# Warm-up products and weight rooms in the opening, spare memory for weights and gated-attention loads, rounded masks and values two blocks behind in a one-core decoder step

## The chip, the cores and the metric

The kernel runs on one core of one Trainium2 chip. The metric is device time in microseconds (us) of one execution, as the median of several. A core has a matrix engine (TensorE, in the profile PE for its products and PEld for its weight loads), a vector engine (VectorE, DVE), a scalar engine (ScalarE, ACT), GpSimd (POOL), and SyncE (SP), which here only issues DMAs. Each engine works through its own instructions in the order in which the program holds them.

## The reference

One step of a decoder layer, for a prompt of 1024 rows and for 8 sequences of 8 new rows over a paged cache of 8192 positions (64 blocks of 128 positions for each sequence):

```
n = rmsnorm(h, g_mix);  u = n @ w_in          # one projection; columns: gq gk gv gg ga mq mkv mkr
z = ga @ gla_w_a2 + gla_b_a                   # gate of the gated linear attention
o_gla = gla_chunked(gq, gk, gv, log_sigmoid(z) / 16, state)
cq = rmsnorm(mq);  q = rope(rmsnorm(cq @ mla_w_qup));  ckv = rmsnorm(mkv);  krope = rope(rmsnorm(mkr))
k, v = latent_to_kv(ckv, krope, mla_w_kvup)
o_mla = prompt_attention(q, k, v)             # causal, prompt;  sample_attention over the paged cache for the 64 sample rows
h = h + concat(o_gla, o_mla) @ w_o
h = h + conv_ffn(rmsnorm(h));  h = h + (p @ ple_w_proj) * sigmoid(rmsnorm(h) @ ple_w_gate)
```

`ga`, `mq`, `mkv` and `mkr` together are 432 columns of `w_in`, called the latents below (`NL` = 432).

## The kernel before

Everything is float32. A product of full precision is made of three products of rounded halves: an operand x is split into a high part (`act.copy` into the type fp32r, F32R in the code) and a low part (x minus the high part, on DVE or POOL), and high x high, high x low and low x high are added up in PSUM (`mm3`, L139 to L141).

Two streams of work are interleaved. `cache_stream()` walks the 64 cache blocks of the sample attention (tiles `craw`, `ctp`, `cTh`/`cTl`, `ks`, `csr`, `mt`, `cpv`). `dense()` does all other work as generators that yield between steps: the opening and the first half of the prompt (`prompt_half(0)`), the second half (`prompt_half(1)`), gated linear attention (`gla_sample`, `gla_prompt`), `prompt_attention`, the output projection, then, from about 1340 us on, the feed-forward layer and the tail. A table `PACE` says how much dense work goes beside a cache block. The program written so is then put in order, for each engine, by the Tile scheduler at build time, which places instructions by its own estimates of when operands are ready; so an edit in one place can move instructions far from it.

The parts that the change touches:

- **The opening.** `sample_x` (L336) loads and normalises the 64 sample rows and transposes them (`pt`, `transpose_split` L128) into `xTs`. `load_lat` (L259) loads the 432 latent columns of `w_in` in eight pieces of 128 rows through a `stage` buffer, of which there are three: a piece is loaded (L266), its high part copied by ACT (L267), its low part made by DVE or POOL in turn (L271), and only then is the buffer free for a piece three further on. `sample_u` (L344) multiplies the sample rows with these weights (`ps_sm`), `proj_lat` (L741) each prompt tile (`ps_lt`), k by k with all three products. Both come out of `mm_lat` (L274, matmul L278). The sample rows then go through a chain of their own: latents, `ps_qs` (L390), norms and rotation on DVE and ACT (`q_finish`), transposes `pt_q` (L416), products `ps_qp` (L420).
- **The mix chunks.** `proj` multiplies 512 prompt columns with a chunk of 128 columns of `w_in` (`ps_pj`). Its weights come by `load_mix` (L252) and `wload` (L143) in two pieces through `stage`; the tile `w` that takes the parts has three buffers (pool `wp`). `PLAN` (L30) says which chunks come where: in the second half chunk 0 first, then the q and kv products (`ps_q`, `ps_kv`), then chunks 1 to 3. The sample rows' `xTs` and the gains `gmix` are not read any more by then.
- **Gated attention.** L1375 opens two pools, `g` for the sample rows and `g2` for the prompt. Their tiles lie in memory that the first part gave back, so their first loads wait for its last readers. `ps_z` (L1007) needs the gate's loads `gaT<-dga` (L1002).
- **Prompt attention.** Scores of 128 rows against 512 columns; in the blocks on the diagonal a matmul with a bfloat16 identity (`identb`) as weights adds the mask `maskq` or `maskk` to them (L1281, L1311; 64 each). Behind each block's scores ACT takes the exponential `p`, ACT or DVE rounds it to `ph`, POOL makes the low part `pl` (L1316 to L1318, three buffers each); the product with the values `o` (L1323 to L1326) comes one block behind the scores.

## Time and profile before

| | before |
|---|---|
| time, median of 3 runs | 2216.69 us (2213.21 to 2216.88) |
| span of the profiled execution | 2211.1 us |
| PE busy | 2126.7 us, 96% |
| PEld / DVE / ACT / POOL busy | 87% / 75% / 62% / 56% |
| share of the chain that ended last | PE 79%, DVE 7%, ACT 5%, DMA 3%, POOL 3%, issue 2% |

The profile is one execution; the median lies 5.6 us above its span. Busy time counts an instruction from its start to its modelled end, and matmuls overlap, so the pace of PE is read from start to start. `PEclk` in the tables is the granted clock of PE as a share of the full 2.4 GHz; 0.50 is 1.2 GHz. Two levels occur, so a stretch's mean tells how long each held.

### The profile page before, as it was taken

To read this page: it belongs to the slowest core of one execution; us is meant where nothing else is said; L and a number is where in the kernel's file an instruction comes from. 1 tells how busy PE (TensorE), PEld (TensorE's weight loads), DVE (VectorE), ACT (ScalarE), POOL (GpSimd) and SP (SyncE) were. 2 spreads that over 40 slices of the span, in tenths; PEclk is the share of its full clock that TensorE was granted. 3 is DMA by queue.
4 is the path that set the end of the run, shared out by engine and by line. 5 is a ranking of instruction groups with operands and counts; after the bars stand their busy time and mean duration, and the time that the engine had idled before them with its cause. 6 is when DMAs were issued, how large, how long until landed. Compare 5 with 4: busy or idle time off the path is not lost.

```text
span 2211.1 us, 38379 instructions
## 1 busy us (share of the span) xinstructions
PE 2126.7 (96%) x13460; PEld 1927.2 (87%) x13460; DVE 1668.4 (75%) x2551; ACT 1366.7 (62%) x3724; POOL 1233.9 (56%) x1330
## 2 busy tenths in 40 slices
PE   7999989999999999999999997999999999999999
PEld 6889978878888888887898875999999999888899
DVE  4775667467788888887888788888888886887642
ACT  5676766777778888887777766333333333534631
POOL 5675668576777777778455557756566562011100
PEclk9999999999999999999999998999999999999999
DMA  5343235412342222221522222332232325777321
GB/s 185 106 144 108 78 119 156 141 54 69 105 120 61 63 74 61 61 56 46 171 77 69 74 77 82 101 102 90 92 95 91 101 91 191 240 218 237 101 71 39
DMA packets 204418, 233.07 MB, mean 105 GB/s; under 512 B 42422, under 2 KB 146339, under 8 KB 204227
## 3 DMA queue, kind: packets, MB, share of 16 engines
q1 hardware_dynamic: 188259, 179.49, 26.0%
q0 software_dynamic: 14736, 46.67, 7.4%
q10 hardware_dynamic: 1232, 4.46, 0.5%
q8 instruction: 108, 1.77, 0.3%
q14 instruction: 83, 0.68, 0.1%
HBM read 188.00 MB, written 42.52 MB: 104 GB/s over the span
## 4 chain that ended last, share of the span: by engine, by line
PE 79%; DVE 7%; ACT 5%; DMA 3%; POOL 3%; issue 2%; SPq 0%; DVEq 0%; POOLq 0%; ACTq 0%
PE ps_gu L140 7%; PE ps_gu L141 7%; PE ps_gu L139 7%; PE ks L139 5%; PE ks L141 4%; PE ks L140 4%; PE ps_dn L140 3%; PE ps_dn L141 3%; PE ps_dn L139 3%; PE cpv L646 2%; PE ctp L522 2%; PE ps_lt L278 2%; PE ps_pj L139 2%; DVE css L565 1%; PE ps_pj L140 1%
## 5 line engine op out<-in xcount | busy, mean ns | idle before, releaser
L560 ACT ACTIVATE csq<-ks 128x256 f32<-128x256 f32 x1040 | 392.7, 400 | 91.1 <-PE ks L141 80.2
L565 DVE TENSOR_REDUCE css<-csq 128x16 f32<-128x1024 f32 (+1 forms) x264 | 315.7, 1196 | 61.2 <-ACT csq L560 58.2
L115 ACT CAST wh<-st 128x512 fp32r<-128x512 f32 x176 | 108.4, 619 | 189.0 <-PE ps_gu L140 168.7
L139 PE MATMUL ks<-mv0h,cTh 128*128 128x320 f32 (+1 forms) x520 | 171.0, 331 | 8.8 <-ACT sn L562 4.6
L139 PE MATMUL ks<-mv1h,cTh 128*128 128x320 f32 (+1 forms) x520 | 169.6, 328 | 7.8 <-ACT sn L562 3.5
L605 POOL TENSOR_TENSOR chl<-craw,chl 128x1024 fp32r<-128x1024 f32 x64 | 141.6, 2213 | 55.2 <-ACT chl L603 53.0
L140 PE MATMUL ks<-mv1l,cTh 128*128 128x320 f32 (+1 forms) x520 | 153.1, 296 | 0.0
L140 PE MATMUL ks<-mv0l,cTh 128*128 128x320 f32 (+1 forms) x520 | 152.0, 294 | 0.0
L141 PE MATMUL ks<-mv0h,cTl 128*128 128x320 f32 (+1 forms) x520 | 147.6, 297 | 0.9 <-DVE cTl L116 0.8
L141 PE MATMUL ks<-mv1h,cTl 128*128 128x320 f32 (+1 forms) x520 | 148.0, 298 | 0.1
L116 DVE TENSOR_TENSOR wl<-st,wh 128x512 fp32r<-128x512 f32 x132 | 119.0, 903 | 26.3 <-ACT wh L115 26.3
L631 POOL TENSOR_TENSOR phl<-sn,phl 128x512 fp32r<-128x512 f32 (+1 forms) x64 | 85.5, 1335 | 84.8 <-ACT phl L630 84.3
L116 POOL TENSOR_TENSOR wl<-st,wh 128x512 fp32r<-128x512 f32 x44 | 69.4, 1578 | 102.9 <-ACT wh L115 102.9
L140 PE MATMUL ps_dn<-o 128*128 128x512 f32 x308 | 120.1, 390 | 0.4 <-DVE o L116 0.4
L141 PE MATMUL ps_dn<-o 128*128 128x512 f32 x308 | 120.2, 390 | 0.0
L116 DVE TENSOR_TENSOR cTl<-ctp,cTh 128x512 fp32r<-128x512 f32 (+1 forms) x136 | 90.0, 662 | 37.8 <-ACT cTh L115 36.8
L139 PEld LDWEIGHTS ks<-mv0h,cTh 128*128 128x128 f32 x520 | 97.9, 188 | 23.2 <-ACT sn L562 9.4
L562 ACT COPY sn<-ks 128x64 f32<-128x64 f32 x520 | 116.7, 224 | 0.0
L139 PEld LDWEIGHTS ks<-mv1h,cTh 128*128 128x128 f32 x520 | 99.0, 190 | 20.1 <-ACT sn L562 7.9
L1318 POOL TENSOR_TENSOR pl<-p,ph 128x512 fp32r<-128x512 f32 (+1 forms) x96 | 97.5, 1020 | 30.3 <-DVE ph L1317 21.2
L139 PE MATMUL ps_dn<-o 128*128 128x512 f32 x308 | 112.1, 390 | 0.0
L141 PE MATMUL ps_gu<-xrh,wl 128*128 128x320 f32 x352 | 108.7, 309 | 0.0
(670 smaller groups left out, 7871.4 us busy)
## 6 DMA issues: line engine op xcount, KB each, us to landing
raw<-ds SPq DMA_DIRECT2D x77, 256.0 KB
raw<-ffn_w_down SPq DMA_DIRECT2D x66, 256.0 KB
stage<-w_in SPq DMA_DIRECT2D x48, 256.0 KB
st<-ffn_w_gate SPq DMA_DIRECT2D x44, 256.0 KB
st<-ffn_w_up SPq DMA_DIRECT2D x44, 256.0 KB
wr<-ffn_w_down SPq DMA_DIRECT2D x44, 256.0 KB
ds<-cv SPq DMA_DIRECT2D x21, 512.0 KB
oraw<-doT SPq DMA_DIRECT2D x16, 256.0 KB
```

What stands on the lines that cost most here:

```text
L115: cast = act.copy(hi, src)
L116: res = (lo_eng or dve).tensor_tensor(lo, src, hi.bitcast(F32), ALU.subtract)
L139: pe.matmul(ps, ah, bh, start=first, stop=False)
L140: pe.matmul(ps, ah, bl, start=False, stop=False)
L141: return pe.matmul(ps, al, bh, start=False, stop=last)
L278: pe.matmul(ps, x, w, start=first, stop=last)
L560: act.activation(sq[:, f * 256:f * 256 + 256], ks[:, 0:256], AF.Square)
L562: act.copy(o.sn[:, g0 + i, :], ks[:, 256:320])
L565: dve.tensor_reduce(o.ss[:, g0 + i + 1 - n:g0 + i + 1, :].rearrange("p i h -> p (i h)"), sq2[:, :n].rearrange("p i (h n) -> p (i h) n", n= ...
L605: pool.tensor_tensor(ch[:, c0:c1, 128:256], src, ch[:, c0:c1, 0:128].bitcast(F32), ALU.subtract)
L631: pool.tensor_tensor(phl[:, :nt, 64:128], sb, phl[:, :nt, 0:64].bitcast(F32), ALU.subtract)
L1318: pool.tensor_tensor(pl[:, c0:], p[:, c0:], ph[:, c0:].bitcast(F32), ALU.subtract)
```

## The change

1. **Opening.** A tile of ones `warm` (bfloat16, in the memory of `csq`) feeds 13 matmuls of 512 columns ahead of the sample rows' transposes and 8 behind them; their result is not read. The eight raw pieces of the latent weights get rooms of their own in the buffers `craw` and `csq` of the cache stream, which has not begun. All low parts are made by DVE. The first prompt tile is turned before the sample products; `sample_u` and `proj_lat` take all products of one kind before the next, and the next tile is turned between the second and the third kind.
2. **Second half.** Chunks 1 and 3 take their weight parts in `xTs` and `gmix` (`spare`) rather than in `w`; chunk 1's are loaded before the q and kv weights (`ahead`).
3. **Gated attention.** `g2` is opened before `g`, and its first tiles are placed at once.
4. **Prompt attention.** Identity and masks are fp32r; a mask is built in float32 and rounded by one more POOL copy. `ph` and `pl` have four buffers, the values' products come two blocks behind.

```diff
-    def load_mix(c0, lo_eng=pool):
-        w = wtile().rearrange("p (k s c) -> p k s c", k=8, s=2)
+    def load_mix(c0, lo_eng=pool, spare=False):
+        if spare:
+            w, hl = None, tuple(xp.tile([P, 8, P], F32R, tag=t, name="wx") for t in ("xTs", "gmix"))
...
+            raw = rooms[k] if rooms else wp.tile([P, NL], F32, tag="stage", name="stage", bufs=3)
...
+        if rooms:
+            for k in range(8):
+                raw_in(k)
+            return (hi, lo), low
...
-        for k in range(8):
-            for s in range(2):
+        for s in range(2):
+            for k in range(8):
                 mm_lat(ps[:, :NL], xTs[:, k, :], w[s][k], k + s == 0, k + s == 8)
...
-            for k in range(8):
-                mm_lat(ps[:, :NL], xTh[:, k, ii], w[0][k], k == 0, False)
-                mm_lat(ps[:, :NL], xTh[:, k, ii], w[1][k], False, False)
-                mm_lat(ps[:, :NL], xTl[:, k, ii], w[0][k], False, k == 7)
+            for n, (x, s) in enumerate(((xTh, 0), (xTl, 0), (xTh, 1))):
+                for k in range(8):
+                    mm_lat(ps[:, :NL], x[:, k, ii], w[s][k], n + k == 0, n + k == 9)
+                if n == 1 and between is not None:
+                    between()
...
+            warm = cp.tile([P, 512], BF16, tag="csq", name="warm", bufs=2)
+            dve.memset(warm, 1.0)
...
+            last = warm_up(13)
+            with tc.issue_after(sample_x(last)):
+                last = warm_up(8)
...
+        if hf:
+            for c in PLAN[2][:1]:
+                ahead[c] = load_mix(c * P, spare=True)
         rank()
...
-        identb = ap.tile([P, P], BF16, name="identb", tag="identb", bufs=1)
+        identr = ap.tile([P, P], F32R, name="identr", tag="identr", bufs=1)
...
-            for j in range(nj + 1):
+            for j in range(nj + 2):
...
-                if j > 0:
+                if j > 1:
                     jj, c0, ph, pl = q.pop(0)
...
-            g, g2 = (s2.enter_context(tc.tile_pool(name=nm, bufs=2, reuse_waits="tile")) for nm in ("g", "g2"))
+            g2, g = (s2.enter_context(tc.tile_pool(name=nm, bufs=2, reuse_waits="tile")) for nm in ("g2", "g"))
+            for nm, shape, n in (("gaT", [17, P], 2), ("qk", [P, 4, P], 2), ("gv", [P, 512], 3)):
+                g2.tile(shape, F32, tag=nm, name=nm, bufs=n)
```

How the instructions stand now, at three places. From the feed-forward layer on the order is the same on every engine; ahead of it all engines are ordered anew.

SP, the opening, before (`lat` and `xin` are prompt tiles, `stage` the weights' buffer):

```order
L338 DMA xin_s<-x_sample 64x1024
L339 DMA gmix<-g_mix 128x1024
L759 DMA lat<-x_prompt 128x1024
L266 DMA stage<-w_in 128x432 x3
L759 DMA lat<-x_prompt 128x1024
L78 DMA gtile<-mla_g_qa 128x256
```

and after:

```order
L355 DMA xin_s<-x_sample 64x1024
L356 DMA gmix<-g_mix 128x1024
L778 DMA lat<-x_prompt 128x1024
L272 DMA lraw<-w_in 128x432 x6
L272 DMA lraw_223<-w_in 128x432 x2
L778 DMA lat<-x_prompt 128x1024
```

All eight pieces now stand together where three stood; the other five stood between small loads, further down the queue.

PE, from the sample rows' `ps_qs` to their transposes `pt_q`, the first rows of that stretch, before:

```order
L390 MATMUL ps_qs<-wql,cqT_s 128x384
L278 MATMUL ps_lt<-w,xTh 128x432 x2
L278 MATMUL ps_lt<-w,xTl 128x432
L278 MATMUL ps_lt<-w,xTh 128x432 x2
L278 MATMUL ps_lt<-w,xTl 128x432
L278 MATMUL ps_lt<-w,xTh 128x432 x2
L278 MATMUL ps_lt<-w,xTl 128x432
L139 MATMUL ps_pj<-xTh,w 128x512
```

and after:

```order
L408 MATMUL ps_qs<-wql,cqT_s 128x384
L132 MATMUL pt<-ident,xin 128x128 x2
L295 MATMUL ps_lt<-chl,xTh 128x432 x2
L295 MATMUL ps_lt<-w,xTh 128x432 x12
L295 MATMUL ps_lt<-w,xTl 128x432 x8
L295 MATMUL ps_lt<-chl,xTh 128x432 x4
L295 MATMUL ps_lt<-w,xTh 128x432 x4
L426 MATMUL pt_wk<-ident,wkr 64x128 x8
L140 MATMUL ps_pj<-xTh,w 128x512
```

In both, 24 `ps_pj`, eight `pt_wk` and eight `ps_sm` of 256 columns lie between `ps_qs` and `pt_q`; of the latents' products `ps_lt` there were nine and are now 30.

SP, the last q and kv loads of the second half and what stands behind them, before (`stage<-w_in 128x4x128` is half of a chunk's weights; `mla_w_qup`, `mla_w_kvup` are those of q and kv; the others are stores and small loads of the latents):

```order
L157 DMA stage<-mla_w_qup 128x384 x3
L479 DMA newc<-ckvs 8x128
L157 DMA stage<-mla_w_kvup 128x512
L865 DMA ckv_p<-lat 128x128
L157 DMA stage<-mla_w_kvup 128x512
L157 DMA stage<-w_in 128x4x128
L480 DMA newk<-krs 8x32
L866 DMA krope_p<-lat 128x32
L157 DMA stage<-w_in 128x4x128 x2
```

and after, from the end of the latent weights:

```order
L272 DMA stage<-w_in 128x432 x5
L158 DMA stage<-w_in 128x4x128 x4
L158 DMA stage<-mla_w_qup 128x384
L908 DMA ckv_p<-lat 128x128
L909 DMA krope_p<-lat 128x32
L908 DMA ckv_p<-lat 128x128
L497 DMA newc<-ckvs 8x128
L909 DMA krope_p<-lat 128x32
L498 DMA newk<-krs 8x32
L908 DMA ckv_p<-lat 128x128
```

Chunk 1's two loads have moved from behind the last kv load to directly behind chunk 0's, ahead of all q and kv loads.

## Rows read from the trace of the kernel before

**Rows 1.** The page: busy us of each engine (share of the span), instructions.

```profile
PE 2126.7 (96%) x13460; PEld 1927.2 (87%) x13460; DVE 1668.4 (75%) x2551; ACT 1366.7 (62%) x3724; POOL 1233.9 (56%) x1330
```

**Rows 2.** Waits of PE: engine, tile, line, releaser: us in total, times, longest us.

```profile
PE pt L132 <- DVE xin_s L125: 8.1, 1, 8.1
...
PE mt L626 <- DVE mt L623: 5.1, 4, 2.6
...
PE ps_pj L139 <- ACT w L115: 3.8, 1, 3.8
PE pt_q L416 <- DVE qt L328: 3.5, 1, 3.5
...
PE ps_z L1007 <- DMA gaT<-dga: 2.2, 1, 2.2
...
PE o L1326 <- POOL pl L1318: 0.4, 1, 0.4
```

**Rows 3.** Stretches: from:to, length, busy us (instructions) by engine, granted clock, DMA share, GB/s.

```profile
0.00:24.00 24.00, 12.31 (x46) 10.52 (x46) 12.70 (x19) 13.20 (x25) 11.26 (x37) 1.00 0.68 218
...
46.00:70.00 24.00, 19.62 (x96) 15.71 (x95) 18.97 (x56) 15.08 (x50) 18.16 (x27) 0.79 0.56 171
...
280.00:290.00 10.00, 4.65 (x19) 3.46 (x19) 4.78 (x8) 4.95 (x14) 2.29 (x3) 0.66 0.72 207
...
349.00:358.00 9.00, 6.37 (x26) 5.83 (x25) 5.82 (x14) 4.46 (x13) 5.24 (x8) 0.62 0.85 237
```

**Rows 4.** Stretches of 2 us in the opening, columns as above.

```profile
8.00:10.00 2.00, 1.11 (x8) 0.93 (x8) 0.37 (x2) 1.97 (x5) 0.65 (x2) 1.00 1.04 403
...
12.00:14.00 2.00, 2.00 (x10) 1.57 (x8) 1.46 (x3) 0.22 (x2) 0.96 (x2) 1.00 0.02 6
```

**Rows 5.** SP's queue in the opening: start, us, line, DMA, count.

```profile
2.55 1.38 SPq L266 DMA_DIRECT2D stage<-w_in  x3
...
20.61 0.33 SPq L266 DMA_DIRECT2D stage<-w_in  x1
```

**Rows 6.** PE in the opening: start, us, line, product, shapes, count.

```profile
22.32 0.56 PE L278 MATMUL ps_lt<-chl,xTh 128*128 128x432 f32 x1
22.68 0.56 PE L278 MATMUL ps_lt<-w,xTl 128*128 128x432 f32 x1
...
29.00 0.35 PE L278 MATMUL ps_lt<-w,xTl 128*128 128x432 f32 x1
29.19 0.36 PE L278 MATMUL ps_lt<-w,xTh 128*128 128x432 f32 x1
...
46.17 0.39 PE L139 MATMUL ps_pj<-xTh,w 128*128 128x512 f32 x1
```

**Rows 7.** PE, the sample rows' chain: last of ps_qs, first of pt_q; idle before, releaser.

```profile
44.22 0.34 PE L390 MATMUL ps_qs<-wql,cqT_s 128*128 128x384 f32 x1
...
57.28 0.80 PE L416 MATMUL pt_q<-ident,qt 64*64 64x64 f32 x8 [3.54 <-DVE qt L328]
```

**Rows 8.** DVE ahead of the wait at 349 us.

```profile
345.50 0.29 DVE L176 TENSOR_TENSOR rqb<-qt,ropep 128x128 f32<-128x128 f32 x1
...
346.04 3.24 DVE L177 TENSOR_TENSOR rqb<-qt,ropep 128x128 f32<-128x128 f32 x1
```

**Rows 9.** POOL beside it.

```profile
346.58 2.54 POOL L116 TENSOR_TENSOR w<-stage,w 128x512 fp32r<-128x512 f32 x2
```

**Rows 10.** PE, one mask of the prompt attention between its neighbours.

```profile
703.10 0.33 PE L1309 MATMUL S<-ql,kh 97*128 97x384 f32 x1
703.27 0.23 PE L1311 MATMUL S<-maskk,identb 128*128 128x128 bf16 x1
...
703.57 0.39 PE L1323 MATMUL o<-ph,vo 128*128 128x512 f32 x1
```

**Rows 11.** Weight loads by line: count, busy, mean ns of one, idle before.

```profile
L1312 PEld LDWEIGHTS S<-qh,kl 97*128 97x128 f32 x96 | 19.1, 199 | 1.1
...
L1311 PEld LDWEIGHTS <-identb 128*128 128x128 bf16 x64 | 6.3, 98 | 7.6 <-issue 6.9
```

More of the change, by code (lines that the diff above doesn't have):

```diff
@@ L136, in transpose_split @@
             split(hi, lo, pt[:, :, :rows])
+        return m.ins
     def mm3(ps, ah, al, bh, bl, first=True, last=True):
@@ L232, in step_kernel @@
     wp = den.enter_context(tc.tile_pool(name="wp", bufs=3))
-    xTs = xp.tile([P, 8, P], F32R, name="xTs")
-    gmix = xp.tile([P, D], F32, name="gmix")
+    xTs = xp.tile([P, 8, P], F32R, name="xTs", tag="xTs")
+    gmix = xp.tile([P, D], F32, name="gmix", tag="gmix")
     w_in = A["w_in"][0]
@@ L333, in q_finish, with sample_x @@
         return q
-    def sample_x():
+    def sample_x(first):
         x = wk.tile([P, D], F32, tag="xin", name="xin_s")
@@ L340, in sample_x @@
         norm_rows(wk, x[:R], R, gmix)
-        transpose_split(pm, x, R, lambda c0: (xTs[:, c0:c0 + 4, 0:R], xTs[:, c0:c0 + 4, R:2 * R]))
+        with tc.issue_after(first):
+            return transpose_split(pm, x, R, lambda c0: (xTs[:, c0:c0 + 4, 0:R], xTs[:, c0:c0 + 4, R:2 * R]))
     def sample_u(u, w):
         ps = pm([P, 512], "ps_sm")
-        for k in range(8):
-            for s in range(2):
+        for s in range(2):
+            for k in range(8):
                 mm_lat(ps[:, :NL], xTs[:, k, :], w[s][k], k + s == 0, k + s == 8)
@@ L774, in next_x, with turned_in, warm_up @@
                 xs_.append(norm_rows(wk, x, P, gmix))
+        def turned_in(i):
+            transpose_split(pd, xs[i], P, lambda c0: (xTh[:, c0:c0 + 4, i * P:(i + 1) * P],
+                                                      xTl[:, c0:c0 + 4, i * P:(i + 1) * P]))
         if hf == 0:
-            sample_x()
+            warm = cp.tile([P, 512], BF16, tag="csq", name="warm", bufs=2)
+            dve.memset(warm, 1.0)
+            pw = pm([P, 512], "ps_warm")
+            def warm_up(n):
+                for _ in range(n):
+                    m = pe.matmul(pw, warm[:, 0:P], warm, start=True, stop=True)
+                return m.ins
+            last = warm_up(13)
+            with tc.issue_after(sample_x(last)):
+                last = warm_up(8)
             load_x()
-            wl = load_lat([chl[0][:, 2 * k:2 * k + 2, 0:NL // 2] for k in range(4)])
+            rooms = [cp.tile([P, 8, P], F32, tag="craw", name="lraw", bufs=3).rearrange("p a c -> p (a c)") for _ in range(3)]
+            rooms.append(cp.tile([P, 2, 512], F32, tag="csq", name="lraw2", bufs=2).rearrange("p a c -> p (a c)"))
+            wl, low = load_lat([chl[0][:, 2 * k:2 * k + 2, 0:NL // 2] for k in range(4)],
+                               rooms=[x[:, a:a + NL] for x in rooms for a in (0, 512)])
             load_x()
+            xs.append(norm_rows(wk, loaded[0], P, gmix))
+            with tc.issue_after(last):
+                turned_in(0)
+            for k in range(8):
+                low(k, dve)
             load_constants()
@@ L783, in prompt_half @@
             sample_u(u, wl)
-        for i in range(5):
+            yield 0.9
+        for i in range(1 if hf == 0 else 0, 5):
             if hf > 0:
@@ L797, in prompt_half @@
                     cqT = sample_latents(u)
-            if i > 0:
-                transpose_split(pd, xs[i - 1], P, lambda c0, i=i - 1: (xTh[:, c0:c0 + 4, i * P:(i + 1) * P],
-                                                                       xTl[:, c0:c0 + 4, i * P:(i + 1) * P]))
-            if hf == 0 and i > 1:
-                proj_lat(i - 2, wl)
+            if hf == 0:
+                if i < 4:
+                    proj_lat(i - 1, wl, lambda: turned_in(i))
+            elif i > 0:
+                turned_in(i - 1)
             yield 0.9
@@ L866, in norm_latents @@
             sp.dma_start(A["krope_p"][tt, :], l[:, 384:416])
+        ahead = {}
         def mix(chunks, G=None):
@@ L871, in mix @@
                 if c is not None:
-                    w = load_mix(c * P)
+                    w = ahead.pop(c, None) or load_mix(c * P, spare=hf > 0 and c in PLAN[2][::2])
                     st = proj(w, P, G[:, c - 8] if c >= 8 else None)
```

41 lines of the change are left out of this document (25 added, 16 removed).

## The prediction

> **What bounds the kernel now.** I read the page first: TensorE (PE) is busy for 96% of the span [rows 1], so time can come only from the few places where it stands still, or from where its matmuls run at the lower clock. Next, its waits, longest first [rows 2]. Five of them lie at places that the change edits: 8.1 us at the very start, 3.8 us for a chunk's weights, 3.5 us for the sample rows' queries, 2.2 us for the gate's loads, 0.4 us for a low part in the prompt attention. Then stretches around the waits, for the granted clock [rows 3]. Each of the longer ones is followed by matmuls at 1.2 GHz. A stretch's mean clock says for how long: at 46 to 70 us it is 0.79, so (1 - 0.79) x 2 x 24 = 10.1 us at half; at 280 to 290 us 0.66, so 6.8 us; at 349 to 358 us 0.62, so 6.8 us. Work done at half would need half that time, so a wait that goes takes up to 3.4 to 5 us more with it. The opening is an exception to this view: its clock column says 1.00 [rows 3], yet products of 432 columns start 0.36 us apart at 22 us and 0.19 us apart at 29 us [rows 6]. By that pace PE is at half until about 23.4 us.
>
> The sum is made on the profiled span, 2211.1 us. The median, 2216.7 us, is 5.6 us above it, and I carry the same offset over.
>
> **Opening.** SP issues three weight pieces at 2.55 us and the eighth at 20.61 us [rows 5]: with three buffers each later piece waits for a copy and a subtraction. Between, the DMA runs at 403 GB/s and then at 6 GB/s [rows 4]. With eight rooms all 1.77 MB (8 x 128 x 432 x 4 bytes) stand in one row of the queue; at 403 GB/s that is 4.4 us, some 3 us more than the first three need, so everything is there at about 12 us. The 13 warm-up products fill time in which PE waits anyway (8.1 us, [rows 2]) and cost nothing as long as the sample rows come no earlier; the eight behind the transposes lie in the gap until the next operands are split, at 0.23 to 0.43 us each (512 columns, in proportion to the 0.19 and 0.36 us of 432 [rows 6]). PE has some 12.3 us of busy time ahead of 24 us [rows 3], 6 at full clock, and is then packed until 46.17 us, where the first chunk starts [rows 6]. Fed and warm from 11.5 us, that point would come at 11.5 + 6 + 22.8 = 40.3. But DVE now makes all eight low parts, and two row norms stand among them, so I expect tile 0's parts about 2 us late: **-4 us**, between -2 and -6.
>
> **The sample rows' chain.** The last `ps_qs` starts at 44.22 us; the queries come out of the norms at 57.28, 13.1 us later [rows 7]. Beside it PE had nine `ps_lt` and 24 `ps_pj`, and ran dry for 3.5 us. The order of the changed kernel puts 30 `ps_lt` there: 21 more at 0.195 us [rows 6] are 4.1 us, more than the hole. The wait should vanish, and with it the 10.1 us at half clock (5 us of loss), 8.5 us in all. Against that, `ps_qp` now stands right behind `pt_q` and waits about 1 us for a copy, and what hides the chain is just about as long as the chain: if DVE or ACT is late by more than 0.6 us (4.1 - 3.5) a wait is back, and a longer one brings back the half clock. **-7.5 us**, between -3 and -8.5.
>
> **Second half.** Here PE waits 3.8 us for chunk 1's weights [rows 2], then has 6.8 us at half [rows 3], together 3.8 + 3.4 = 7.2. The two loads move ahead of all q and kv loads, and the parts go to memory that nobody reads then, so they need no `w` buffer. What is moved past them is q's and kv's weights, late by two loads, two casts on ACT and two subtractions on POOL (2.54 us for two, [rows 9]); `ps_q` comes behind chunk 0's 24 products, which covers that. Chunk 2 then gets the `w` buffer. **-7 us**, between -4 and -7.2.
>
> **Gated attention.** The prompt's first loads no longer stand behind those of the sample rows' state, and their tiles lie in the memory that is freed first. The 2.2 us for `gaT` [rows 2] go: **-2.2 us**, between 0 and -2.2.
>
> **Masks.** From the mask's start to the next product's start but one is 0.30 us; a product of 384 columns alone takes 0.17 [rows 10]. So a mask costs 0.13 us now, 128 times. As F32R it streams 128 columns, a third of 0.17, 0.06 us, and its weights load in 0.199 instead of 0.098 us [rows 11]. If that load is hidden the mask costs 0.06 (-9 us in all); if it is fully exposed 0.06 + 0.2 = 0.26 (+16.6 us). I take the middle near to today's value, since today a mask also pays more than its streaming, namely the load of its neighbour: 0.12 each, **-1 us**. The two extra POOL copies are once and hidden.
>
> **Values two blocks behind.** POOL's low part gets one more block of scores as cover. The wait on it in the trace is 0.4 us [rows 2]: **-0.5 us**, between -1 and 0.
>
> **The new order.** From the feed-forward layer on the order is unchanged on every engine, 0. Ahead of it the scheduler has dealt all instructions anew, the cache blocks too. What such a deal can hold is seen at 346 us: a DVE operation lasts 3.24 us where one of the same shape takes 0.29 [rows 8], just while POOL subtracts weights for 2.54 us [rows 9]; PE waits 2.6 us for what is queued on DVE behind it [rows 2] and goes to half clock for 6.8 us, 2.6 + 3.4 = 6 us in all. The new order may lose that one (-6) or draw two more (+12). The old order was one draw and so is the new, but the parts that the change moves lie beside such work: **+4 us**.
>
> The Trainium skill, page "SBUF — State Buffer", section "SBUF: two separate sides", says that DVE and GpSimd share one port pair, that an operation of DVE with two SBUF inputs and one of GpSimd that reads SBUF take it in turn for the whole instruction, and that the loser fully blocks. The row agrees in kind: the 3.24 us end when POOL's two subtractions end.
>
> **Sum:** -4 - 7.5 - 7 - 2.2 - 1 - 0.5 + 4 = -18.2; 2216.7 - 18.2 = **2198.5**, say 2199 us.
>
> **Rivals.** (A) The opening and the chain give half back: DVE has the low parts, two norms and the splits of tile 0 in one line, PE waits for it and falls to half clock again, and the queries still end last. For it: PE takes its work in order, so one late split holds all behind it; against it: tile 0 is the only one in that position. The opening then gives nothing and the chain -3: 2198.5 + 4 + 4.5 = 2207.
> (B) Slower: the new order pairs DVE operations with POOL's subtractions at more places. One costs 6 us as at 349 us; the gain of 18.2 plus 4.4 is used up by four beyond those in my +4: 2198.5 + 24 = 2222.5, and from there on it decides. For it: the change moves chunk weights, which POOL subtracts, next to the latents' norms on DVE; and low parts that POOL made are on DVE now. Against it: the trace has one such wait of this size in 1340 us.
> (C) The masks lose. A hidden load becomes an exposed one: 0.199 - 0.098 = 0.10 us [rows 11], 128 times, 12.9 us, instead of my -1: 2198.5 + 13.9 = 2212.4. Against it: a bf16 load has idle time before it [rows 11], so loads are not what a mask waits for; and the next load was an F32R one before as well. This is the rule that speaks against the change: the Trainium skill, page "TensorE: Matmul & The Clock Gate", section "Weight-path perf modes", says that the fast weight load is on for 128 weights of a type other than FP32, which an identity in F32R would give up. The rows agree on the size, 98 against 199 ns.
> (D) The change does not do what it says: the loads stand early but the memory behind them is given back late (the rooms by the tiles before, `xTs` by its last reader), or the stalls come back at the next step. All terms 0: 2217.
> (E) More goes than I counted: the opening at its bound and the wait at 349 us gone too: 2198.5 - 2 - 10 = 2186.5.
>
> **How the numbers follow.** A difference below 0.2% (4.4 us: 2212.3 to 2221.1) is about what a measurement of this kernel can tell from no change. Forecast with its own spread, 2191 to 2205: 0.54. A 0.17. B 0.09. C 0.07, on the border, counted as no change. D 0.05. E 0.08. So faster 0.54 + 0.17 + 0.08 = 0.79, the same 0.12, slower 0.09. The range goes from E's end, 2186, to 2212, where C begins: it leaves out B, C, D and some of E, about 0.2.
>
> **What would show it.** In the changed profile: SP's eighth weight piece issued before 8 us, products of 432 columns at 0.19 us from about 10 us on, and the first chunk's product at about 42 us instead of 46.2. No wait of `pt_q` above 0.5 us and a clock of 1.00 from 24 to 70 us. No wait of `ps_pj` for `w` at the second half's start, and none of `ps_z` for `gaT`. A mask's spacing of about 0.12 us. The matmuls of the feed-forward layer unmoved but for their start, earlier by some 18 us. I am wrong if new waits of 2 us or more, followed by half clock, appear between 70 and 1340 us (B), if mask loads of 0.2 us stand in front of waiting PE (C), or if the opening's DVE rows show PE waiting for `xTl` (A).

## The result and the profile after

| | before | after |
|---|---|---|
| time, median of 10 runs | 2216.05 us (2213.21 to 2218.72) | 2223.44 us (2218.7 to 2227.44) |
| ratio to before, 95% interval | 1 | 1.0032 (1.0022 to 1.0041) |
| span of the profiled execution | 2211.1 us | 2220.8 us |

The change makes the kernel slower, by some 7 us; a gain of 18.2 us was forecast. The two spans differ by more, 9.7 us: the profiled execution of before is a short one, 5 us under its median, that of the changed kernel 2.6 us. The page's row of busy times hardly differs from that of before [rows 1], PE is again busy for 96%:

```profile
PE 2128.3 (96%) x13481; PEld 1940.2 (87%) x13481; DVE 1677.6 (76%) x2556; ACT 1366.3 (62%) x3724; POOL 1226.7 (55%) x1328
```

So PE does the same work and stands still, or runs at half clock, elsewhere. Its waits (tile, line, releaser: us in total, times, longest):

```profile
PE ctp L540 <- DMA craw<-cache_ckv,idx: 10.1, 2, 9.5
...
PE pt_gvs L882 <- DVE gsf L309: 5.0, 3, 3.3
...
PE pt L132 <- DVE xin_s L125: 2.6, 1, 2.6
...
PE ps_gv L140 <- ACT sqk L986: 2.2, 1, 2.2
PE ctp L540 <- ACT qp L439: 2.0, 1, 2.0
...
PE pt L132 <- DVE xTs L116: 1.7, 1, 1.7
```

The waits that the prediction counted on are gone from this list: `pt_q` for `qt`, `ps_pj` for `w` and `ps_z` for `gaT` [rows 2]. The longest is new, 9.5 us for a gather of the cache, and so are those of `pt_gvs`, `ps_gv` and `ctp` for `qp`. Stretches of the changed kernel (columns as in [rows 3]):

```profile
58.00:66.00 8.00, 5.99 (x30) 4.84 (x29) 7.51 (x26) 5.02 (x11) 5.03 (x15) 0.57 0.62 175
96.00:128.00 32.00, 27.44 (x155) 25.15 (x154) 25.49 (x41) 20.96 (x66) 20.97 (x24) 0.89 0.33 107
280.00:290.00 10.00, 10.00 (x62) 8.76 (x61) 8.47 (x22) 6.11 (x21) 3.43 (x4) 1.00 0.54 153
...
1051.00:1066.00 15.00, 5.48 (x27) 5.31 (x26) 4.16 (x6) 3.20 (x13) 5.12 (x10) 0.66 1.01 382
```

At 280 to 290 us PE is now full at a clock of 1.00, where it had 4.65 us and 0.66 [rows 3]. At 58 to 66, at 96 to 128 and at 1051 to 1066 us it has what it lacks elsewhere.

To see where the two run apart, I gave every matmul the mean spacing of its kind at full clock in both traces (the warm-up products nothing), added these up as work, in us, and looked when equal amounts of it were done:

```
work done, us   before at   after at   lead (-) or lag (+)
    20             37.2       38.0        +0.8    opening
    40             64.5       58.5        -6.0    the chain's wait is gone
    80            105.1      103.2        -1.9    half clock from 58.9, ctp waits for qp
   120            148.2      152.9        +4.7    pt_gvs, ps_gv
   200            227.7      230.6        +2.9
   240            267.5      274.7        +7.2    xTl 1.0 us, half clock
   260            294.1      295.2        +1.1    second half's weights early
   400            441.9      442.6        +0.7    gaT early
   580            636.3      634.5        -1.8
   960           1017.8     1024.8        +7.0    prompt attention
  1000           1068.9     1079.5       +10.7    the late gather
  1260           1352.2     1361.4        +9.2    feed-forward layer from here: unchanged
```

Three gains stand where they were forecast: 6.7 us between work 20 and 40 (forecast 7.5), 6.1 us between 240 and 260 (7), 2.1 us between 380 and 400 (2.2). All the rest is loss, about 24 us. These are single executions: ten other traces whose order is still that of before at work 80 lie there between 1 us ahead of before's trace and 4 us behind it, with a median of 2, so a row of the table is certain to some 3 us only, and the lag it shows is more likely too large than too small.

**The opening.** SP's queue in the changed kernel (start, us):

```profile
2.54 5.68 SPq L272 DMA_DIRECT2D lraw<-w_in  x8
8.50 0.33 SPq L778 DMA_DIRECT2D lat<-x_prompt  x1
```

The weights come as forecast: eight loads in one row. But the prompt tiles are loaded through the same queue. Tile 1 stood here before:

```profile
3.97 0.55 SPq L759 DMA_DIRECT2D lat<-x_prompt  x1
```

so tile 1 is issued 4.5 us later, and tiles 2 and 3 by 2.5 and 4.4 us. And PE (idle time before and its releaser in brackets):

```profile
1.52 4.33 PE L806 MATMUL ps_warm<-warm 128*128 128x512 bf16 x13 [1.52 <-DVE warm L801]
8.42 0.46 PE L132 MATMUL pt<-ident,xin_s 64*128 64x64 f32 x4 [2.57 <-DVE xin_s L125]
10.58 0.46 PE L132 MATMUL pt<-ident,xin_s 64*128 64x64 f32 x4 [1.70 <-DVE xTs L116]
10.98 3.49 PE L806 MATMUL ps_warm<-warm 128*128 128x512 bf16 x8
...
15.20 1.03 PE L295 MATMUL ps_sm<-w,xTs 128*128 128x432 f32 x4
...
25.59 0.22 PE L368 MATMUL pt_us<-ident,u_s 64*16 64x64 f32 x1 [1.41 <-DVE u_s L165]
...
27.27 2.49 PE L295 MATMUL ps_lt<-w,xTh 128*128 128x432 f32 x8 [0.80 <-ACT xTh L115]
```

The sample rows' transposes came as one run of eight before and now are split, the second four waiting 1.7 us for the first four's parts on DVE; without the second warm-up products (an experiment below) they are one run again, so the likely reason, not shown, is the PSUM bank that these products hold in the same pool. Then the eight second warm-up products run, at half clock, for 3.5 us in front of tile 0. The first product starts at 15.2 us where it started at 10.65 us (idle before it: DVE's `xTs`). From 14.5 us on the clock is full, which is what the eight were there for; but at 24.2 us PE has run out of work, waits 1.4, 0.3 and 0.8 us (for the sample rows' `u_s` and `ptf` from DVE, then for tile 1's `xTh` from ACT), and is at half again for 3.4 us.

**One step on in the chain.** The wait for the queries is gone, but the next link waits instead:

```profile
57.83 0.68 PE L444 MATMUL pt_qr<-ident,q 64*128 64x64 f32 x8
...
61.83 1.12 PE L540 MATMUL ctp<-ident,craw 128*128 128x128 f32 x4 [2.01 <-ACT qp L439]
```

`ctp` is released by the copy of `qp`; before, 5.4 us of other products stood between `ps_qp` and it. Around the 2.0 us the clock is at half (0.57 at 58 to 66 us). They are not what it fell behind: by the trace it is at half from 58.9 us, 0.9 us before this wait begins, to 65.7 us. What PE did before that is 4.5 us of narrow work, transposes and products of 64 and 128 columns, with one wait of 0.7 us for `qT_s`.

**117, 146 and 354 us.** DVE operations, the last of them first in an undisturbed place; POOL beside it; what PE waited for:

```profile
91.69 0.28 DVE L178 TENSOR_TENSOR rqb<-qt,ropep 128x128 f32<-128x128 f32 x1
...
115.13 1.29 DVE L176 TENSOR_TENSOR rqa<-qt,ropep 128x256 f32<-128x256 f32 x1 [0.63 <-POOL qt L348]
116.34 1.38 DVE L177 TENSOR_TENSOR rqb<-qt,ropep 128x128 f32<-128x128 f32 x1
117.64 2.25 DVE L178 TENSOR_TENSOR rqb<-qt,ropep 128x128 f32<-128x128 f32 x1
...
120.72 0.28 DVE L309 TENSOR_TENSOR gsf<-ps_sm,gsf 64x128 f32<-64x128 f32 x1
```

```profile
117.52 2.22 POOL L623 TENSOR_TENSOR chl<-craw,chl 128x1024 fp32r<-128x1024 f32 x1
```

```profile
121.06 0.36 PE L882 MATMUL pt_gvs<-ident,gsf 64*128 64x64 f32 x1 [3.33 <-DVE gsf L309]
```

`rqb` takes 2.25 us instead of 0.28 while POOL subtracts `craw` for 2.2 us; the two operations ahead of it take 1.29 and 1.38 instead of 0.43 and 0.28 us, also beside POOL. The next operations on DVE, up to `gsf`, are late by that, and PE waits 3.3 us and goes to half clock. This is the mechanism of rival B and of [rows 8, 9], at a new place. The Trainium skill, page "SBUF — State Buffer", section "SBUF: two separate sides", has it that DVE and GpSimd take a shared port pair in turn; the two rows agree.

It is there twice more, each time with other links between DVE and PE. DVE, POOL and PE at 146 us, then at 354 us:

```profile
146.17 2.43 DVE L179 TENSOR_TENSOR qt<-rqa,rqb 128x256 f32<-128x256 f32 x1
...
146.13 2.19 POOL L623 TENSOR_TENSOR chl<-craw,chl 128x1024 fp32r<-128x1024 f32 x1
...
152.32 0.39 PE L140 MATMUL ps_gv<-w,xTh 128*128 128x256 f32 x1 [2.15 <-ACT sqk L986]
```

```profile
354.35 1.72 DVE L344 TENSOR_TENSOR qt<-qt,qrs 128x512 f32<-128x512 f32 x1
...
354.25 1.28 POOL L649 TENSOR_TENSOR phl<-sn,phl 128x512 fp32r<-128x512 f32 x1
...
357.95 0.39 PE L140 MATMUL ks<-mv1h,cTh 128*128 128x256 f32 x1 [2.56 <-ACT sn L580]
```

At 146 us `qt` takes 2.43 instead of 0.43 us; its store `dq<-qt` goes out behind it, ACT waits for the store before it writes the next tile into the same memory, and PE waits for ACT. At 354 us `qt` takes 1.72 instead of 0.69 us, and `qrs` ahead of it 1.12 instead of 0.17; ACT, and behind it PE, wait for what DVE does next. So three of PE's waits of over 2 us between 70 and 400 us come this way, 3.3, 2.2 and 2.6 us, where before had one, the 2.6 us at 349 us.

**1051 us.** The cache gathers on POOL, then SP, then PE, then how long the three gathers of that stretch took from issue to landing:

```profile
1042.22 0.95 POOL L491 DMA_INDIRECT craw<-cache_ckv,idx  x1 [0.31 <-issue]
...
1052.41 1.00 POOL L491 DMA_INDIRECT craw<-cache_ckv,idx  x1 [0.58 <-POOL qbd1l L509]
```

```profile
1051.30 2.77 SPq L1605 DMA_DIRECT2D h<-x_prompt  x5
```

```profile
1060.83 1.09 PE L540 MATMUL ctp<-ident,craw 128*128 128x128 f32 x4 [9.52 <-DMA craw<-cache_ckv,idx]
```

```profile
DMA to landing us min/median/max: 4.7/4.9/8.3
```

The prompt attention ends 14 us earlier than before (last `o` product at 1039.0 against 1052.6 us), so SP begins earlier to load the next part's rows: two of 512 KB at 1049.40 us and five more from 1051.30 us. The gather, issued among them, needs 8.3 us instead of 4.7 to 4.9. And PE has nothing else: the output projection waits for its own loads in the same row. 9.5 us of wait, and 0.66 of the clock in these 15 us. The slow landing is the smaller part: the gather is issued at 1052.41 us, 1.1 us after PE has run dry (1051.3), so one of 4.9 us would have left a wait of 6.

### The profile page after: what moved, and what is told of

Same layout as the page of the kernel before. It is cut to its first block, busy times and chain, and to the rows that moved or that the text cites. A ratio compares the mean times of both kernels' runs of the same rounds, so it can differ in the third digit from the quotient of the medians.

```text
span 2220.8 us, 38460 instructions
## 1 busy us (share of the span) xinstructions
PE 2128.3 (96%) x13481; PEld 1940.2 (87%) x13481; DVE 1677.6 (76%) x2556; ACT 1366.3 (62%) x3724; POOL 1226.7 (55%) x1328
## 4 chain that ended last, share of the span: by engine, by line
PE 75%; DVE 10%; ACT 6%; POOL 4%; DMA 3%; issue 3%; SPq 0%; DVEq 0%; POOLq 0%; ACTq 0%
PE ps_gu L142 7%; PE ps_gu L141 7%; PE ps_gu L140 7%; PE ks L140 5%; PE ks L141 4%; PE ks L142 4%; PE ps_dn L141 3%; PE ps_dn L142 3%; PE ps_dn L140 3%; PE cpv L664 2%; DVE css L583 2%; PE ctp L540 2%; ACT csq L578 1%; PE ps_pg L142 1%; PE ps_pg L141 1%
## 5 line engine op out<-in xcount | busy, mean ns | idle before, releaser
L141 PE MATMUL ks<-mv0l,cTh 128*128 128x256 f32 (+1 forms) x520 | 153.4, 297 | 0.0
L142 PE MATMUL ks<-mv0h,cTl 128*128 128x256 f32 (+1 forms) x520 | 149.5, 297 | 0.2 <-DVE cTl L116 0.2
L1368 POOL TENSOR_TENSOR pl<-p,ph 128x512 fp32r<-128x512 f32 (+2 forms) x96 | 97.0, 1015 | 34.1 <-ACT ph L1367 17.5
L140 PE MATMUL ps_gu<-xrh,wh 128*128 128x320 f32 x352 | 108.7, 309 | 0.9 <-ACT xrh L115 0.9
```

What stands on the lines that cost most here:

```text
L140: pe.matmul(ps, ah, bh, start=first, stop=False)
L141: pe.matmul(ps, ah, bl, start=False, stop=False)
L142: return pe.matmul(ps, al, bh, start=False, stop=last)
L1368: pool.tensor_tensor(pl[:, c0:], p[:, c0:], ph[:, c0:].bitcast(F32), ALU.subtract)
```

## The experiments

All ratios are to the kernel before, run on the same chip beside them.

**Each part by itself.** First the kernel before with the hunks of one part of the change.

```diff
+            last = warm_up(13)
...
+            wl, low = load_lat([chl[0][:, 2 * k:2 * k + 2, 0:NL // 2] for k in range(4)],
+                               rooms=[x[:, a:a + NL] for x in rooms for a in (0, 512)])
```

> The kernel before with part 1 alone (warm-up products, rooms, order of products, low parts on DVE). Its order equals the changed kernel's up to about 200 us. Theory P (each loss belongs to a part, since the part puts an instruction where it waits): the waits of the changed kernel at 24 us (pt_us for u_s, 1.4 us), 60 us (ctp for qp, 2.0 us) and 117 us (pt_gvs for gsf, 3.3 us, with 6.8 us at half clock behind it) all come back, the lead over before in useful work falls from -6 us at 58 us to +4 us or so at 150 us, and the end is +1 to +8 us against before. Theory L (the waits are drawn anew by every reordering and belong to no part): the waits at 60 and 117 us are there only if the whole order is the same, so no statement beyond 200 us; the end is anywhere within -6 to +8 us. Forecast of record for this part: -11.5 us (-4 and -7.5).

Measured: 2223.53 us, 1.0041 (1.0028 to 1.0054). The waits of the first 200 us are those of the changed kernel; from the list of PE's waits, the three of `pt_gvs`, of which 3.4 us at 117 us (us in total, times, longest):

```profile
PE pt_gvs L879 <- DVE gsf L306: 5.1, 3, 3.4
```

The lead was -7.2 us at work 40 and a lag of +4.3 at work 140. What the opening and the chain gain is given back within some 110 us.

```diff
+        if hf:
+            for c in PLAN[2][:1]:
+                ahead[c] = load_mix(c * P, spare=True)
```

> The kernel before with part 2 alone (chunk 1's weights early, spare memory). Its order differs from before between about 220 and 450 us only. Theory P: the 3.8 us wait of ps_pj for w at 283 us and the 6.8 us at half clock behind it go, no new wait of over 1 us comes, -5 to -7 us, so about 2210. Theory L: the gain is there, but the reordering between 290 and 450 us draws a new wait with half clock, so -3 to +1 us.

Measured: 2215.43 us, 1.0004 (0.9994 to 1.0014). The wait for `w` is gone; -4.4 us at work 320 and +0.2 at work 400: new waits of 1.5 and 1.9 us at 329 and 332 us, with 3.4 us of half clock, and the unchanged wait for `gaT` was longer (us in total, times, longest), with 6.8 us at half clock behind it, which before had none:

```profile
PE ps_z L1015 <- DMA gaT<-dga: 2.9, 1, 2.9
```

```diff
-            g, g2 = (s2.enter_context(tc.tile_pool(name=nm, bufs=2, reuse_waits="tile")) for nm in ("g", "g2"))
+            g2, g = (s2.enter_context(tc.tile_pool(name=nm, bufs=2, reuse_waits="tile")) for nm in ("g2", "g"))
```

> The kernel before with part 3 alone (the prompt's pool first, its tiles placed at once). Theory P: the 2.2 us wait of ps_z for gaT goes, nothing else changes in kind, -2 us (-3 to 0). Theory L: the order is dealt anew from about 330 us to 1340 us, so beside the 2.2 us gained the stretches of the prompt attention move by up to 6 us either way; -6 to +6 us.

Measured: 2238.19 us, 1.0093 (1.0079 to 1.0108). The wait for `gaT` is gone, as forecast; 20.6 us are lost in many places behind it. The first of them, 430 to 480 us:

```profile
PE ps_b L1150 <- DVE z L1013: 2.0, 1, 2.0
...
PE pa L1178 <- POOL kx L1169: 1.0, 1, 1.0
```

One reorder of two pools that are worth 2 us costs ten times as much. No term of the prediction had that size.

```diff
-                        pe.matmul(S[:, kw - P:kw], identb, maskq, start=False, stop=True)
+                        pe.matmul(S[:, kw - P:kw], identr, maskq, start=False, stop=True)
...
-                if j > 0:
+                if j > 1:
```

> The kernel before with part 4 alone (masks in fp32r, values two blocks behind). Its order is that of before up to about 640 us. Theory P: the prompt attention is slower by itself, by the 5 us that the changed kernel loses between 640 and 1040 us, and at its end the cache gather comes late as at 1051 us in the changed kernel (9.5 us of wait, 10.2 us at half clock); +5 to +12 us. Theory L: the late gather is drawn by the place of the last cache blocks against the attention's end, so it need not be there; -3 to +6 us.

Measured: 2224.30 us, 1.0035 (1.0023 to 1.0046), with the late gather at 1057 us; from the list of PE's waits:

```profile
PE ctp L522 <- DMA craw<-cache_ckv,idx: 8.5, 2, 8.2
```

**Two behind alone.**

```diff
-            for j in range(nj + 1):
+            for j in range(nj + 2):
...
-                if j > 0:
+                if j > 1:
```

> The kernel before with the values two blocks behind and four buffers, and the masks as before. Theory P: the two-behind form makes the attention end earlier against the cache stream, so the late gather (8 to 9.5 us of wait at its end) is there as with both edits: +5 to +9 us against before. If instead the masks make it: no gather wait over 2 us here, and -2 to +3 us. Theory L: the order is dealt anew from about 430 us on, with any outcome from -3 to +20.

Measured: 2222.92 us, 1.0030 (1.0020 to 1.0039); the gather's wait is 2.2 us. So the length of the gather's wait is not the two-behind edit's alone. That there is such a wait at all comes with the edit: of the twenty kernels measured here, none of the ten whose values come one block behind has in its trace a wait of `ctp` for a gather at the attention's end, and all ten with two blocks behind have one, from 0.3 to 10.0 us, five of them over 8 us. Between 1000 and 1120 us PE is idle for 8.3 us in the mean of the former and 12.1 us of the latter. The order sets its size.

What the edit does to the distance between a block's scores and its values' product (96 blocks, from the traces):

```
                      mean us   median us   score blocks in between, mean
before                  4.33       4.12        0.82
two behind alone        5.39       4.86        1.02
changed kernel          5.09       4.60        0.93
```

The program says one block more; the scheduler, by its own estimates, puts 0.1 to 0.2 of one. And the waits that it was to shorten, in the prompt attention, with two behind (for `pl` it was 0.4 us before, [rows 2], for `ph` 0.3 us):

```profile
PE o L1323 <- DVE ph L1317: 2.0, 2, 1.5
PE o L1326 <- POOL pl L1318: 1.7, 2, 1.4
```

Both have grown.

**The opening.** The second warm-up products left out:

```diff
-                last = warm_up(8)
+                pass
```

> The changed kernel without the eight warm-up products behind the sample rows' transposes; its order is otherwise that of the changed kernel up to about 1000 us. Theory W (those eight, 3.5 us at half clock in front of the first tile's transposes, hold the opening up): the first product of the sample rows starts 2 to 3.5 us earlier than 15.2 us, and the lead stays: -2 to -4 us against the changed kernel, 2219 to 2221. Theory V (DVE holds it up: the low part of the sample rows ends at 14.1 us, behind four low parts of weights): the first product starts at 14.1 us or later, the gain is under 1.2 us, and the clock may fall to half for longer: 2222 to 2225.

Measured: 2227.29 us, 1.0048 (1.0034 to 1.0063).

PE's timeline, first product of the sample rows and first of the first chunk:

```profile
10.51 1.81 PE L295 MATMUL ps_sm<-w,xTs 128*128 128x432 f32 x4 [1.78 <-DVE xTs L116]
...
46.99 0.48 PE L140 MATMUL ps_pj<-xTh,w 128*128 128x512 f32 x1
```

The first product comes 4.7 us earlier, at 10.51 us; the first chunk's product at 46.99 instead of 47.73 us. Theory W is right about the place and wrong about the gain, 0.7 us at the first chunk: a wait of 2.5 us at 22.8 us (`ps_lt` for tile 1's `xTh`) and 6.8 us of half clock behind it take the rest. Next, the prompt tiles' loads ahead of the weights:

```diff
-                last = warm_up(8)
+                pass
+            load_x()
+            load_x()
             load_x()
             rooms = [cp.tile([P, 8, P], F32, tag="craw", name="lraw", bufs=3).rearrange("p a c -> p (a c)") for _ in range(3)]
...
-            load_x()
```

> The changed kernel without the eight second warm-up products and with the loads of the second and third prompt tile ahead of the eight weight pieces on SP instead of behind them. Theory T (the opening is bound by the prompt tiles, which the eight weight pieces pushed back on SP: tile 1 from 3.97 to 8.50 us, tile 2 from 11.86 to 14.40, tile 3 from 12.84 to 17.25): the waits between 22 and 27 us and the half clock there shrink, the first chunk's product starts at 42 to 45 us instead of 47.7 (47.0 without the second warm-up). Theory V (DVE's line of norms, low parts and splits bounds it): 46 us or later. Of the total neither says more than that the order is dealt anew: 2215 to 2232.

Measured: 2223.32 us, 1.0042 (1.0029 to 1.0055).

PE's timeline, first product of the first chunk:

```profile
46.93 0.47 PE L140 MATMUL ps_pj<-xTh,w 128*128 128x512 f32 x1
```

46.93 us, as good as the same. Theory T falls as the single bound; here PE waits 2.7 us for tile 0's norm, runs at half for 6.8 us, and waits three times under 1 us, with 3.4 us more at half, between 28 and 37 us. Three different orders of the opening end within 0.8 us of each other. All three have eight `pt_wk` (0.8 us) ahead of this product which before has behind it, so at equal work the changed kernel is 0.8 us behind before's 46.17 [rows 6] and the other two are level with it. What each saves is lost to a wait elsewhere and the half clock behind it.

**The late gather.** More cache blocks beside the attention:

```diff
-PACE = [1.41, 1.088, 1.601, 1.168, 1.142, 0.708, 1.035, 1.027]
+PACE = [1.41, 1.088, 1.601, 1.168, 1.142, 0.708, 1.0, 1.027]
```

> The changed kernel with the pace of the cache stream in the prompt attention 1.00 instead of 1.035 (more cache blocks beside the attention); its order is the changed kernel's up to about 1020 us. Theory G (the 9.5 us wait for the gather at 1051 us comes because the attention ends with the cache stream behind it, and the output projection is not ready): the wait is under 4 us and the half clock of 10.2 us behind it shorter; -8 to -14 us against the changed kernel, 2210 to 2216. Against it: the wait only moves, -2 to +4 us.

Measured: 2224.96 us, 1.0037 (1.0024 to 1.0050). The gather's wait fell from 9.5 to 1.6 us, and another took its place (1040 to 1080 us):

```profile
PE cpv L664 <- POOL phl L649: 5.6, 2, 4.4
...
PE ctp L540 <- DMA craw<-cache_ckv,idx: 1.6, 1, 1.6
```

The wait has moved, the time has not.

**The order itself.** If a reordering can cost 20 us, how much do orders differ with no edit at all? Changing a number of `PACE` slightly leaves the work as it is and makes the scheduler deal the instructions anew. The edits are to the first number (1.46, 1.36, 1.51, 1.56 instead of 1.41), and once to the sixth:

```diff
-PACE = [1.41, 1.088, 1.601, 1.168, 1.142, 0.708, 1.035, 1.027]
+PACE = [1.46, 1.088, 1.601, 1.168, 1.142, 0.708, 1.035, 1.027]
```

> The kernel before with no edit to its work: only the first number of the pace table is 1.46 instead of 1.41, so that the scheduler deals the instructions anew from about 150 to 1100 us. Theory L (before's order is a well-drawn one, picked out of many; any new deal costs): +4 to +20 us, with three or more new waits of over 1 us or stretches at half clock. Theory P (the losses belong to the parts): within -4 to +4 us of before.

Measured: 2212.57 us, 0.9978 (0.9968 to 0.9988). Theory L, that any new deal costs, fell with this: the first new deal is better. Its milder form did not: of the five new deals of before below, the other four are slower than before, by 5 to 14 us. Before's order is a good one among its deals, and the changed kernel is measured at the pace numbers of before. Whether these had been chosen for before's order no run here shows.

> The kernel before with its sixth pace number 0.73 instead of 0.708: the same work, the order dealt anew from about 850 to 1150 us only. If a new deal by itself moves the time by several us either way, as the one from 150 us on did (-4 us): -5 to +8 us, and the waits that move lie inside that stretch. If a new deal as a rule costs: +2 to +8 us.

Measured: 2220.63 us, 1.0022 (1.0012 to 1.0033).

> The changed kernel with the first pace number 1.46 instead of 1.41: the same work, the order dealt anew from about 60 us on. If the losses come from where the parts put an instruction in this one order, they move: the 3.3 us wait at 117 us and the gather's 9.5 us at 1051 us are gone or elsewhere, and the time is anywhere from 2208 to 2235. If the parts themselves lose, the time stays within 2220 to 2228 with waits of the same kind.

Measured: 2236.68 us, 1.0091 (1.0076 to 1.0106). The waits at 97 to 150 us are gone and 14 us of lead over the first changed kernel stand at work 320; 35 us are lost behind that, at other waits (`ps_kv` 4.3 us at 353, `cpv` 5.4 us at 443, `o` 2.7 us at 753 us).

```diff
 # parts 2 and 3 together
+                ahead[c] = load_mix(c * P, spare=True)
...
+            g2, g = (s2.enter_context(tc.tile_pool(name=nm, bufs=2, reuse_waits="tile")) for nm in ("g2", "g"))
```

> The kernel before with parts 2 and 3 together. By the single runs' own gains (part 2 about -6 us at its place, part 3 -2 us at its place) and nothing else: 2208. By the sum of the single runs' totals (+1 and +20.6): 2238. If each deal is its own draw: no rule, 2208 to 2238.

Measured: 2220.78 us, 1.0020 (1.0012 to 1.0029): 16 us less than part 3 alone. The parts' totals do not add up.

**Both kernels in more deals.** The same numbers in before and in the changed kernel:

> The kernel before with the first pace number 1.36, the same work, the order dealt anew from about 70 us on. If the spread of deals explains the result (theory D: what the change loses is the draw of its order, and its parts gain what they take away in place): deals of before and of the changed kernel overlap, and over pairs with equal pace numbers the changed kernel is on the whole 5 to 15 us faster; here 2208 to 2238. If the parts themselves lose (theory P): each deal of the changed kernel is slower than that of before with the same numbers, by about 7 us.

> The kernel before with the first pace number 1.51, the order dealt anew from about 130 us on. As for 1.36: 2208 to 2238 by theory D, and slower than the changed kernel with 1.51; by theory P faster than it by about 7 us.

> The changed kernel with 1.36; its order differs from the changed kernel's between about 60 and 400 us only. By theory D 5 to 15 us faster than before with 1.36, and since the waits at 97 to 150 us belong to one order, they are gone or moved: 2213 to 2225. By theory P slower than before with 1.36 by about 7 us.

> The changed kernel with 1.51; its order differs from the changed kernel's between about 60 and 400 us only. By theory D 5 to 15 us faster than before with 1.51; by theory P slower by about 7 us.

> The kernel before with the first pace number 1.56, the third of the pairs. So far before lies at 2216.0 (1.41), 2212.6 (1.46), 2229.1 (1.36), 2230.0 (1.51), the changed kernel at 2223.4, 2236.7, 2216.4, 2216.8 in the same order: differences +7, +24, -13, -13. Theory D (the draw decides): anywhere from 2208 to 2238, no fixed difference. Theory P (+7 us in each pair) has fallen with two pairs; it would need this one and its mate 7 us apart.

> The changed kernel with 1.56: between 60 and 400 us its order is that of the deal with 1.51 (2216.8 us), behind 900 us it is dealt anew. If the deal of the first half carried the gain of 1.51 over the changed kernel (-6.6 us, the waits at 97 to 150 us), this one keeps it at 400 us; the total is 2210 to 2228 by what comes behind 900 us.

Measured, with the first deal and that of 1.46 (median us; ratio and its interval; difference from the ratios):

```
first number   before                               changed kernel                       difference
1.41           2216.05  1                           2223.44  1.0032 (1.0022 to 1.0041)     +7 us
1.46           2212.57  0.9978 (0.9968 to 0.9988)   2236.68  1.0091 (1.0076 to 1.0106)    +25 us
1.36           2229.08  1.0053 (1.0037 to 1.0070)   2216.37  1.0003 (0.9993 to 1.0012)    -11 us
1.51           2230.03  1.0061 (1.0044 to 1.0078)   2216.81  1.0007 (0.9998 to 1.0017)    -12 us
1.56           2231.52  1.0060 (1.0038 to 1.0082)   2212.45  0.9979 (0.9968 to 0.9990)    -18 us
```

The deals of one kernel lie 19 us (before) and 24 us (changed) apart. The mean of the five differences is -2 us, and with a scatter of 18 us it says nothing about its sign. Nor are they five independent draws: the deals of 1.51 and 1.56 share their order up to some 900 us in either kernel. Theory P, a loss that belongs to the parts, asked for +7 in each pair and has fallen. Of theory D, one half stands: the order decides the total. The other half, that the parts' gain of some 15 us shows on the mean, is not shown. The traces show more. At work 300 (some 340 us; work counted as in the table further up, one execution each) the changed kernel is 9 to 13 us ahead in the four pairs with a new number (again not four independent ones), and 2 us behind in the first pair alone. At the feed-forward layer the five pairs stand at +10, +23, -16, -17 and -22 us. What a better deal looks like, in the changed kernel with 1.56:

```profile
96.00:128.00 32.00, 31.40 (x197) 28.48 (x197) 25.89 (x52) 26.17 (x87) 22.47 (x27) 1.00 0.37 120
1035.00:1051.00 16.00, 9.69 (x51) 9.03 (x50) 9.64 (x15) 9.79 (x26) 10.37 (x11) 0.68 0.85 285
```

At 96 to 128 us PE is busy 31.40 of 32 us at full clock (27.44 and 0.89 above). The gather at the attention's end is late there too. This version and before with 1.46 beat both kernels, the better of the two by 0.2%.

## Why the prediction was wrong

- **Opening, -4.** Failed: +0.8. The loads did what was said. "Cost nothing" was wrong for the warm-up products: the second eight take PE's time in front of real work, which starts 4.7 us earlier without them, though only 0.7 us of that is left at the first chunk. What the first 13 were to do for the clock was lost in the waits of 2.6 and 1.7 us behind them; the eight did raise it. PE was to be fed from 11.5 us and then packed; it was fed from 14.3 us, and from 24.2 us it waited 2.5 us for the sample rows and tile 1, a term that the sum put at nothing. The tiles that the eight loads push back on SP were not counted either, but with them in front (an experiment above) the opening was no better than without the second warm-up. Rival A named the wrong wait: none of these is for `xTl`.
- **Chain, -7.5.** Right in place (-6.7), not in the sum: its last link became late next, 2.0 us, and 6.8 us at half clock came around that. The prediction looked one step on (`ps_qp`, 1 us; measured 0.7), not two.
- **Second half, -7; gated attention, -2.2.** Right in place (-6.1 and -2.1). That part 2 is not the only way to the former is seen in the opening alone, which has the same 5.7 us there without part 2.
- **Masks, -1.** Right that it is small; the sign is not resolved. A mask between its neighbours and a weight load of its line in the changed kernel:

```profile
702.94 0.23 PE L1361 MATMUL S<-maskk,identr 128*128 128x128 f32 x1
...
703.17 0.40 PE L1376 MATMUL o<-pl,vo 128*128 128x512 f32 x1
```

```profile
L1361 PEld LDWEIGHTS S<-maskk,identr 128*128 128x128 f32 x64 | 12.2, 191 | 0.6
```

From the mask to the next product but one it is 0.23 us with products of 256 columns. From the matmul ahead of a `maskk` to the second behind it, among scores of the same width and without a wait between them, the medians went from 601 to 581 ns with 512 columns, from 478 to 464 with 384, from 362 to 352 with 256, and from 300 to 335 with 128. The load takes 191 ns instead of 98 [rows 11] and is hidden but behind the narrowest scores; over the 64 `maskk` that adds up to about nothing. Rival C, 0.10 us for each of 128, fell. It rested on the Trainium skill's rule of the fast weight load (page "TensorE: Matmul & The Clock Gate", section "Weight-path perf modes"), on for 128 weights of a type other than FP32. The two loads differ as if F32R counted as FP32.
- **Two behind, -0.5.** Failed: +6.7 alone. The scheduler undoes most of the edit. The late gather at the attention's end, which the sum did not have, comes with it in every deal; the rest is a new deal.
- **The new order, +4 between -6 and +12.** This is the step that failed: in this deal everything outside the three gains in place lost about 24 us, where the sum had +4 and at most +12. I priced one kind of wait and let at most two more of it appear. Two more did (three of over 2 us against one). What was put at nothing is the other kinds: a copy behind its own product (2.0 us at 60), a gather behind other loads (9.5 us at 1051), the opening's waits, and the half clock beside most of them. The measured spread of deals is 19 to 24 us, some three times the largest term of the sum. Rival B's price, 2222.5 us, was nearly the result, and that was luck: its mechanism was there, but two such waits more, not the four beyond two that its price needs. Its sign, new waits of 2 us or more followed by half clock, was the right one to look for.

Whether the sum of the local gains, about 15 us, is worth anything in the total over many orders is open. The measured result is one pair; of the five pairs two lost and three gained.

## What to carry to other kernels

Where a scheduler orders the program at build time, an edit is two things: its local effect and a new deal of everything behind it. Before crediting or blaming an edit that is worth a few us, deal the order anew several times without it and see how far the times spread. A loss that comes back in every deal with the edit and in none without it, as the late gather does, belongs to the edit; one that moves belongs to the deal. A wait that is removed should be followed along its own chain to the link that is late next, and a filler ahead of real work costs its place in line.

## What the hardware showed that was not expected

The same wait, in the same order, is not always followed by the same stretch at half clock. The kernel before has 10.1 us of it behind the 3.5 us wait at 54 us [rows 3]. The kernel before with part 2 alone, whose matmuls are in the same order up to about 250 us, has the same wait of 3.5 us and in this stretch a clock of 0.70:

```profile
46.00:70.00 24.00, 19.54 (x90) 15.70 (x89) 18.59 (x55) 14.38 (x49) 17.20 (x27) 0.70 0.55 163
```

that is 14.4 us within the stretch (and the half clock goes on beyond it, to 72.7 us). Over the eleven traces with this order there, the wait is 3.5 to 3.8 us, and the half clock 10.2 us long in two of them, 13.7 in four and 17.1 in five. So the profiled spans of one kernel differ by some us, and a difference of 3 us between two profiles is no finding.

Nor does the clock fall behind long waits alone. In the opening of the changed kernel it was at half after waits of 1.4, 0.3 and 0.8 us within 3.1 us (with part 1 alone, 1.1, 0.3 and 0.7 us there were not followed by half clock), and at 58.9 us it fell behind narrow transposes and products with one wait of 0.7 us among them.
